# A hybrid layer of Strassen products on one core: a bank of its own for one product, a normalisation on ScalarE, and a sixth slot

## The chip, the core and the metric

The kernel runs on one core of a Trainium2 chip. The metric is the device time of the whole launch in microseconds (us), as the median of several runs; lower is better. A core has five engines with an instruction queue each: TensorE (PE in the rows) multiplies matrices, VectorE (DVE), ScalarE (ACT) and GpSimd (POOL) work elementwise, and SyncE (SP) only issues DMA transfers. Each queue is served in order, so that an instruction that waits holds up all that stand behind it on its engine. TensorE writes its results into eight banks of PSUM, 128 partitions of 512 fp32 each; the others read them there.

## What is computed

One layer over 1024 tokens of 1024 channels, in fp32: a norm, one wide input projection (7680 columns, 512 of them for `v`), three token mixers, three output projections with gates, a last projection, a residual and a norm.

```python
h = _rmsnorm(x, g)                       # 1024 tokens x 1024
parts = h @ w_in                         # u, v, z_A | x_B, B, C, z_B | x_C, z_C | g_A, g_B, g_C
# mixer A: spatial gating in chunks of 128 tokens
u = jax.nn.gelu(u)
v = _layernorm(jax.nn.gelu(v), ln_g, ln_b)
w_m = jnp.where(causal, w_s, 0.0)
sg = jnp.einsum('gts,bnsgc->bntgc', w_m, vc) + b_s.T[:, :, None]
y_A = u * sg                             # then * silu(z_A)
# mixer B: gated convolution over 3 tokens; mixer C: causal pooling over 2, 4, 8, 16 tokens
# each y * silu(z), times its own matrix, times sigmoid(g); the sum times w_out, plus x; last RMSNorm
```

## The kernel before, in words

**Products.** Every fp32 product is three matmuls of a reduced type: each operand is split into a high and a low part (`split_to`: ScalarE casts the high part, VectorE or GpSimd subtracts for the low one), and `mm3` adds high x high, high x low and low x high (lines 90 to 92) in one bank. On top of it stands the Winograd form of Strassen's method: x, transposed, is cut into four blocks A11 to A22 and four combinations S1 to S4, kept split for the whole main loop; the weights of a pair of 128-column blocks are cut likewise, with T1 to T4 worked out on VectorE. A pair then takes seven products instead of eight, listed in `PRODUCTS`, each of 12 matmuls of 512 columns. From pair 2 on (`PLAIN = 2`), the product A12 x B21 of two neighbouring pairs is again done as seven products of half the size, the "j" steps, whose results `p2_q` VectorE puts together (`joint`).

**The main loop** (lines 539 to 623) runs over 28 pairs: ten of gates ("g") and mixer A ("a") in turn, then mixers B and C with the rest of the gates. In rows of an order, `p37` is the bank of the 37th step, `ch43` and `cl43` the split weights of the 43rd, `T1_n5` the first combination of pair 5, and `o0_4`, `o1_4` the two output tiles of pair 4 (128 channels x 1024 tokens). A pair's steps are (A11,B11) into bank `px`, (S1,T1) into `py_`, (S2,T2), (S3,T3), (A22,T4), (S4,B22). `block` adds a bank and another part into half of an output tile and applies the activation. The two places that matter are these:

```python
px = product(("n", 0), more=True)
...
block(o0, lohalf, px, both[p], f0)       # VectorE reads px
...
nc.scalar.copy(out=u2, in_=product(("n", 2), px))   # (S2,T2) is added onto px
```

**Mixer A.** `v` is projected first, and its gelu put to DRAM. In the pair ahead of an "a" pair, `spatial` loads the weights `wsr`, masks them on GpSimd, splits them into `wss` and loads 128 channels of `v` for all tokens as `vr` (eight tiles of 128 x 128); `spatial_norm` subtracts the mean and multiplies by the deviation's inverse `lr` on VectorE (line 467), multiplies and adds the row gain and bias on GpSimd and splits the result into `vh`, `vl`. In the "a" pair, `spatial_mm` multiplies and ScalarE adds the bias into `st`; `gate` transposes `st` on TensorE into the banks `st_0` and `st_1`, multiplies them into `o0` on VectorE and stores it. `gate` is kept as `late` and called near the end of the next pair.

**Order and slots.** A tile scheduler, not the program's text, settles the order on each engine, from the text's order, the slots and a timeline of its own; the order is fixed when the kernel is built. Tiles of one tag share `BUFS[tag]` slots, taken in turn: "q" (512 fp32 a partition) six, "m" (1024 fp32) five. A tile waits until the slot's earlier user is done. The output tiles, `vr`, `vh`, `vl`, `st`, x and, in the last part, the residual rows `res0` to `res7` are all "m".

**The last part** does the output projection for four pairs of 128-token rows, again with seven products; GpSimd adds parts of them into `res` (loaded from x), VectorE adds the last and normalises, and SP stores. The order is `res1`, `res0`, `res3`, `res2`, `res5`, `res4`, `res7`, `res6`; the last one's last quarter is split in two products, `pl0` and `pl1`. Two of the "m" slots hold other tiles then, so three are left for `res`.

## Time and profile before

| | |
|---|---|
| median of 3 runs | 879.81 us (877.88 to 882.89) |
| the profiled execution | 879.07 us; span of its instructions 877.3 us |
| TensorE busy, granted clock | 831.0 us (95% of the span); 0.983 of full on average |
| VectorE busy | 628.5 us (72%) |
| ScalarE busy | 343.4 us (39%) |
| GpSimd busy | 382.0 us (44%) |
| moved by DMA | 99.56 MB, mean 113 GB/s |

Busy shares are averages over stages with different limits. TensorE is the engine to follow here, since it is busy nearly throughout: what counts is where it waits, for whom, and at which clock it works. A granted clock of 1.00 is the full 2.4 GHz, 0.5 would be 1.2 GHz throughout; a value between is a mean over a stretch. An idle time in square brackets is that of the engine just before the instruction, with the one that released it.

### The profile page before, as it was taken

How to read it: one execution, taken by the hardware profiler on the slowest of the kernel's cores; microseconds unless marked ns; L12 is line 12 of the kernel's file. 1: busy time of each engine (PE TensorE's matmuls, PEld its weight loads, DVE VectorE, ACT ScalarE, POOL GpSimd, SP SyncE). 2: the span in 40 equal slices, each digit the busy share in tenths (PEclk: the TensorE clock that was granted, in tenths of full speed). 3: DMA queues.
4: the chain of work that ended last, by engine and by line, in shares of the span. 5: the costliest groups of instructions: out<-in, count | busy, mean ns of one | idle time of the engine just before them, and what ended most of it. 6: DMA issues, size and time to landing. Idle time of an engine off the chain costs nothing.

```text
span 877.3 us, 11162 instructions
## 1 busy us (share of the span) xinstructions
PE 831.0 (95%) x3950; PEld 693.7 (79%) x3950; DVE 628.5 (72%) x1033; ACT 343.4 (39%) x671; POOL 382.0 (44%) x347
## 2 busy tenths in 40 slices
PE   7999989898989999999999999999999999898992
PEld 6787878787878888888888888888878888785882
DVE  6867776777676778769676767777546745797985
ACT  4435434344443424223235444445433301343431
POOL 6743543645555535344452213143000353548874
PEclk9999999999999999999999999999999999999996
DMA  7402332232313122021221313123498553421044
GB/s 288 157 37 72 107 122 96 63 142 61 144 60 145 49 72 96 25 96 49 72 99 49 139 40 140 73 99 121 154 323 294 173 183 113 151 73 48 5 164 143
DMA packets 33879, 99.56 MB, mean 113 GB/s; under 512 B 3488, under 2 KB 9632, under 8 KB 33824
## 3 DMA queue, kind: packets, MB, share of 16 engines
q1 hardware_dynamic: 27920, 83.90, 27.9%
q10 hardware_dynamic: 5904, 14.96, 4.5%
q8 instruction: 31, 0.51, 0.2%
q14 instruction: 24, 0.20, 0.1%
HBM read 73.68 MB, written 25.17 MB: 113 GB/s over the span
## 4 chain that ended last, share of the span: by engine, by line
PE 74%; DVE 11%; DMA 6%; POOL 5%; issue 2%; ACT 2%; POOLq 0%; DVEq 0%; SPq 0%; ACTq 0%
PE p L90 19%; PE p L91 18%; PE p L92 18%; PE py L751 10%; DMA rawo<-in_units_dram 1%; DVE rq L83 1%; DVE vr L467 1%; POOL S_a L83 1%; DMA x<-in_x_dram 1%; POOL res L83 1%; PE pv L92 1%; DVE wss L83 1%; PE pv L90 1%; PE pv L91 1%; PE po L90 1%
## 5 line engine op out<-in xcount | busy, mean ns | idle before, releaser
L83 POOL TENSOR_TENSOR cl<-raw,ch 128x512 fp32r<-128x512 f32 x58 | 82.3, 1421 | 162.5 <-PE p L92 59.2
L83 DVE TENSOR_TENSOR cl<-T_n,ch 128x512 fp32r<-128x512 f32 x112 | 76.2, 682 | 51.4 <-PE p L91 44.9
L86 ACT CAST ch<-T_n 128x512 fp32r<-128x512 f32 x112 | 65.6, 586 | 94.3 <-PE p L91 48.4
L83 DVE TENSOR_TENSOR o<-p,u 128x512 f32<-128x512 f32 x86 | 58.2, 684 | 24.1 <-PE p L92 23.8
L86 ACT CAST ch<-raw 128x512 fp32r<-128x512 f32 x71 | 43.7, 618 | 44.0 <-PE p L91 33.8
L90 PE MATMUL p<-S2h,ch 128*128 128x512 f32 x112 | 46.4, 414 | 12.0 <-DVE o L83 11.6
L83 DVE TENSOR_TENSOR cj<-T_j,cj 128x256 fp32r<-128x256 f32 x52 | 33.3, 642 | 31.9 <-ACT cj L86 31.9
L86 ACT CAST cj<-T_j 128x256 fp32r<-128x256 f32 x52 | 21.1, 406 | 65.5 <-PE p L91 54.6
L91 PE MATMUL p<-S2l,ch 128*128 128x512 f32 x112 | 45.2, 404 | 0.0
L92 PE MATMUL p<-S2h,cl 128*128 128x512 f32 x112 | 45.1, 402 | 0.0
L557 ACT ACTIVATE o<-o 128x512 f32<-128x512 f32 x48 | 30.0, 631 | 37.9 <-DVE o L83 37.7
L90 PE MATMUL p<-A11h,ch 128*128 128x512 f32 x112 | 44.3, 396 | 0.3 <-ACT ch L86 0.3
L92 PE MATMUL p<-A11h,cl 128*128 128x512 f32 x112 | 43.8, 391 | 0.6 <-POOL cl L83 0.6
L90 PE MATMUL p<-A22h,ch 128*128 128x512 f32 x112 | 43.7, 391 | 0.0
L91 PE MATMUL p<-A22l,ch 128*128 128x512 f32 x112 | 43.7, 391 | 0.0
L90 PE MATMUL p<-S3h,ch 128*128 128x512 f32 x112 | 43.7, 391 | 0.0
L90 PE MATMUL p<-S1h,ch 128*128 128x512 f32 x112 | 43.7, 391 | 0.0
L91 PE MATMUL p<-A11l,ch 128*128 128x512 f32 x112 | 43.7, 391 | 0.0
L91 PE MATMUL p<-S1l,ch 128*128 128x512 f32 x112 | 43.7, 391 | 0.0
L91 PE MATMUL p<-S3l,ch 128*128 128x512 f32 x112 | 43.7, 391 | 0.0
L91 PE MATMUL p<-S4l,ch 128*128 128x512 f32 x112 | 43.6, 389 | 0.0
L90 PE MATMUL p<-S4h,ch 128*128 128x512 f32 x112 | 43.6, 389 | 0.0
(474 smaller groups left out, 2543.9 us busy)
## 6 DMA issues: line engine op xcount, KB each, us to landing
raw<-in_units_dram SPq DMA_DIRECT2D x56, 512.0 KB, 3.3
gate<-o ACTq DMA_DIRECT2D x24, 512.0 KB, 2.7
gt<-gate SPq DMA_DIRECT2D x24, 512.0 KB, 4.4
rawp<-in_units_dram SPq DMA_DIRECT2D x12, 512.0 KB, 4.4
yr<-y SPq DMA_DIRECT2D x12, 512.0 KB, 4.5
x<-in_x_dram SPq DMA_DIRECT2D x8, 512.0 KB, 6.7
y<-o SPq DMA_DIRECT2D x8, 512.0 KB, 2.8
rawo<-in_units_dram SPq DMA_DIRECT2D x8, 512.0 KB, 4.0
```

The costliest lines, as they stand in the source:

```text
L83: eng.tensor_tensor(out=o, in0=a, in1=b, op=op)
L86: nc.scalar.copy(out=hi, in_=src)
L90: nc.tensor.matmul(ps, lhsT=wh, rhs=bh, start=first, stop=False, skip_group_check=shared)
L91: nc.tensor.matmul(ps, lhsT=wh, rhs=bl, start=False, stop=False, skip_group_check=shared)
L92: nc.tensor.matmul(ps, lhsT=wl, rhs=bh, start=False, stop=last, skip_group_check=shared)
L467: nc.vector.tensor_scalar(out=vr[:, i, :], in0=vr[:, i, :], scalar1=mv[:, i, 0:1], scalar2=lr[:, i:i + 1], op0=ALU.subtract, op1=ALU.mult)
L557: nc.scalar.activation(out=dst, in_=dst, func=func)
L751: nc.tensor.matmul(py[h], lhsT=w[:, tsl(c)], rhs=yt[b][h][s][:, c, :], start=c == 0 and w is wh and s == 0, stop=c == CT - 1 and w is wl)
```

## The change

1. Product (S2,T2) goes into a bank of its own. ScalarE copies `px` to a new tile `s1`; VectorE adds the bank and `s1` into `u2`.
2. `v` is normalised by ScalarE: eight activations with the scale `lr` and a bias `lb = -mean * lr`, both pointers to a column. `spatial_norm` is called later in the pair's text, after `spatial_mm`.
3. GpSimd's instructions of 1024 columns in this part are cut into two of 512 (`vr`, the product `o0*o1` of mixers A and B, `a`), and so is the split of `vr`. The low part of `wss` moves from VectorE to GpSimd.
4. `gate` and `pool_mm`, where another pair follows and the pair isn't one of the later gates, are called right ahead of product (S2,T2) in the next pair instead of near its end.
5. "m" has six slots; the scratch tile `junk` of the first norm takes one of them for a while.

```diff
@@ -68,7 +68,7 @@
     dram = ctx.enter_context(tc.tile_pool(name="dram", bufs=1, space=bass.MemoryType.DRAM))
     psum = ctx.enter_context(tc.tile_pool(name="psum", bufs=8, space=bass.MemoryType.PSUM))
 
-    BUFS = {"h": 14, "wc": 18, "raw": 4, "T": 3, "q": 6, "m": 5}
+    BUFS = {"h": 14, "wc": 18, "raw": 4, "T": 3, "q": 6, "m": 6}
 
     def slot(tag, name, shape, dtype=F32):
         return big.tile(list(shape), dtype, name=name, tag=tag, bufs=BUFS[tag])
@@ -174,7 +174,7 @@
         hb[name] = tuple(slot("h", f"{name}{c}", (P, KH, HALF), F32R) for c in "hl")
     v_dram = dram.tile([P, NT, CW], F32, name="v_dram")
     parts = {}
-    junk = const.tile([P, D], mybir.dt.bfloat16, name="junk")
+    junk = slot("m", "junk", (P, D), mybir.dt.bfloat16)
 
     def norm(n):
         i = TOKENS[n]
@@ -441,6 +441,8 @@
     ahead(-1)
     lr = const.tile([P, NT], F32, name="lr")
     rsqrt(mv[:, :, 1], 1.0, LN_EPS, (2, slice(0, NT)), lr)
+    lb = const.tile([P, NT], F32, name="lb")
+    nc.vector.scalar_tensor_tensor(out=lb, in0=mv[:, :, 0], scalar=-1.0, in1=lr, op0=ALU.mult, op1=ALU.mult)
 
     gates = [dram.tile([P, S], F32, name=f"gate{n}") for n in range(24)]
     ys = [[dram.tile([P, S], F32, name=f"y{b}_{j}") for j in range(CT)] for b in range(3)]
@@ -454,7 +456,7 @@
                                 base=0, channel_multiplier=-1)
         wss = slot("q", f"wss{j}", (P, 2, 2 * P), F32R)
         src = wsr.rearrange("p g t -> p (g t)")
-        split_to(wss[:, 0, :], wss[:, 1, :], src)
+        split_to(wss[:, 0, :], wss[:, 1, :], src, nc.gpsimd)
         for r in range(2):
             lo = r * CW + j * P
             nc.scalar.dma_start(out=lnr[:, r, :], in_=rows[0:1, lo:lo + P].broadcast_to([P, P]))
@@ -464,13 +466,15 @@
 
     def spatial_norm(j, wss, lnr, vr):
         for i in range(NT):
-            nc.vector.tensor_scalar(out=vr[:, i, :], in0=vr[:, i, :], scalar1=mv[:, i, 0:1], scalar2=lr[:, i:i + 1],
-                                    op0=ALU.subtract, op1=ALU.mult)
-        tt(nc.gpsimd, vr, vr, lnr[:, 0:1, :].to_broadcast([P, NT, P]), ALU.mult)
-        tt(nc.gpsimd, vr, vr, lnr[:, 1:2, :].to_broadcast([P, NT, P]), ALU.add)
+            nc.scalar.activation(out=vr[:, i, :], in_=vr[:, i, :], func=AF.Identity, bias=lb[:, i:i + 1],
+                                 scale=lr[:, i:i + 1])
         vh = slot("m", f"vh{j}", (P, NT, P), F32R)
         vl = slot("m", f"vl{j}", (P, NT, P), F32R)
-        split_to(vh, vl, vr)
+        for half in range(2):
+            c = tsl(half, KH)
+            tt(nc.gpsimd, vr[:, c], vr[:, c], lnr[:, 0:1, :].to_broadcast([P, KH, P]), ALU.mult)
+            tt(nc.gpsimd, vr[:, c], vr[:, c], lnr[:, 1:2, :].to_broadcast([P, KH, P]), ALU.add)
+            split_to(vh[:, c], vl[:, c], vr[:, c])
         return wss, vh, vl
 
     def spatial_mm(j, wss, vh, vl):
@@ -562,36 +566,40 @@
 
         u2 = slot("q", f"u2_{p}", (P, HALF))
         u3 = slot("q", f"u3_{p}", (P, HALF))
-        px = product(("n", 0), more=True)
+        s1 = slot("q", f"s1_{p}", (P, HALF))
+        px = product(("n", 0))
+        nc.scalar.copy(out=s1, in_=px)
         if nxt[0] == "a":
             sp_next = spatial(nxt[1])
         then(0)
         if p < PLAIN:
-            nc.scalar.copy(out=u2, in_=px)
-            block(o0, lohalf, product(("n", 1)), u2, f0)
+            block(o0, lohalf, product(("n", 1)), s1, f0)
             if p == PLAIN - 1:
                 cut_again(False)
         else:
             block(o0, lohalf, px, both[p], f0)
         py_ = product(("n", 4), more=True)
         then(4)
-        nc.scalar.copy(out=u2, in_=product(("n", 2), px))
+        if late is not None and nxt[0] is not None and not (kind == "g" and j >= 6):
+            late()
+            late = None
+        tt(nc.vector, u2, product(("n", 2)), s1, ALU.add)
         then(2)
         tt(nc.vector, u3, product(("n", 3)), u2, ALU.add)
         block(o1, hihalf, py_, u3, f1)
         then(3)
         if p == 0:
             cut_again(True)
-        if nxt[0] == "a":
-            sp_next = spatial_norm(nxt[1], *sp_next)
         block(o0, hihalf, product(("n", 5)), u3, f0)
         if kind == "g":
             nc.scalar.dma_start(out=gates[2 * j], in_=o0)
         then(5)
         if kind == "a":
             st = spatial_mm(j, *sp)
+        if nxt[0] == "a":
+            sp_next = spatial_norm(nxt[1], *sp_next)
         sp = sp_next
-        if late is not None:
+        if late is not None and kind == "g" and j >= 6:
             late()
             late = None
         block(o1, lohalf, product(("n", 6), py_), u2, f1)
@@ -600,10 +608,12 @@
         if kind == "g":
             nc.scalar.dma_start(out=gates[2 * j + 1], in_=o1)
         elif kind == "a":
-            tt(nc.gpsimd, o0, o0, o1, ALU.mult)
+            for hs in (lohalf, hihalf):
+                tt(nc.gpsimd, o0[:, hs], o0[:, hs], o1[:, hs], ALU.mult)
             late = lambda j=j, st=st, o0=o0: gate(j, st, o0)
         elif kind == "b":
-            tt(nc.gpsimd, o1, o0, o1, ALU.mult)
+            for hs in (lohalf, hihalf):
+                tt(nc.gpsimd, o1[:, hs], o0[:, hs], o1[:, hs], ALU.mult)
             a = slot("m", f"a{j}", (P, S))
             nc.vector.tensor_scalar(out=a, in0=o1, scalar1=cw[:, 3 * j + 2:3 * j + 3], scalar2=cb[:, j:j + 1],
                                     op0=ALU.mult, op1=ALU.add)
@@ -614,8 +624,9 @@
             conv[j] = a
         elif kind == "bz":
             a = conv[j]
-            tt(nc.gpsimd, a, a, o0, ALU.mult)
-            tt(nc.gpsimd, a, a, o1, ALU.mult)
+            for o in (o0, o1):
+                for hs in (lohalf, hihalf):
+                    tt(nc.gpsimd, a[:, hs], a[:, hs], o[:, hs], ALU.mult)
             nc.sync.dma_start(out=ys[1][j], in_=a)
         elif kind == "c":
             pool_weights(j)
```

What this does to the order of instructions, at three places. The first is pair 4 on TensorE, where (S2,T2) begins; before, it followed the half-size product with S1:

```order
L91 MATMUL p40_1668<-S1l_again_959,cj40_1536 128x256
L92 MATMUL p40_1668<-S1h_again_958,cj40_1536 128x256
L90 MATMUL p37_1604<-S2h_141,ch41_1562 128x512
L91 MATMUL p37_1604<-S2l_142,ch41_1562 128x512
L92 MATMUL p37_1604<-S2h_141,cl41_1563 128x512
```

and after the change:

```order
L91 MATMUL p40_1687<-S1l_again_963,cj40_1552 128x256
L92 MATMUL p40_1687<-S1h_again_962,cj40_1552 128x256
L493 MATMUL st0_0_1695<-ident_80,st0_1565 128x128 x4
L493 MATMUL st0_1_1701<-ident_80,st0_1565 128x128 x4
L90 MATMUL p41_1714<-S2h_141,ch41_1578 128x512
L91 MATMUL p41_1714<-S2l_142,ch41_1578 128x512
L92 MATMUL p41_1714<-S2h_141,cl41_1579 128x512
```

The transposes of pair 3's gate now stand ahead of (S2,T2), which writes `p41` instead of adding onto `p37`.

The same stretch on VectorE before: `vr1` is the tile of `v` for the next pair, `o0_4<-p37` the read of `px`:

```order
L467 TENSOR_SCALAR vr1_1625<-vr1_1625,mv_131,lr_804 128x128 x4
L83 TENSOR_TENSOR o1_3_1402<-p28_1431,u2_3_1403 128x512
L467 TENSOR_SCALAR vr1_1625<-vr1_1625,mv_131,lr_804 128x128 x4
L83 TENSOR_TENSOR cl43_1601<-T3_n4_1598,ch43_1600 128x512
L83 TENSOR_TENSOR p2_5_1485<-p36_1585,p2_5_1485 128x256
L83 TENSOR_TENSOR cl44_1630<-T4_n4_1627,ch44_1629 128x512
L83 TENSOR_TENSOR T1_n5_1676<-raw7_1539,raw6_1249 128x512
L83 TENSOR_TENSOR p2_4_1484<-p38_1637,p2_5_1485 128x256
L83 TENSOR_TENSOR wss1_1620<-wsr1_1617,wss1_1620 128x256
L83 TENSOR_TENSOR o0_4_1594<-p37_1604,p2_4_1484 128x512
L83 TENSOR_TENSOR p2_5_1485<-p40_1668,p2_5_1485 128x256
L83 TENSOR_TENSOR cl47_1679<-T1_n5_1676,ch47_1678 128x512
```

and after:

```order
L83 TENSOR_TENSOR cl44_1649<-T4_n4_1646,ch44_1648 128x512
L83 TENSOR_TENSOR T1_n5_1708<-raw7_1555,raw6_1257 128x512
L83 TENSOR_TENSOR o0_4_1611<-p37_1622,p2_4_1500 128x512
L83 TENSOR_TENSOR p2_5_1501<-p40_1687,p2_5_1501 128x256
L83 TENSOR_TENSOR o0_3_1414<-st0_1_1701,o0_3_1414 128x512
L83 TENSOR_TENSOR cl47_1711<-T1_n5_1708,ch47_1710 128x512
L83 TENSOR_TENSOR T2_n5_1728<-raw7_1555,T1_n5_1708 128x512
L83 TENSOR_TENSOR T3_n5_1741<-raw7_1555 128x512
L83 TENSOR_TENSOR u2_4_1613<-p41_1714,s1_4_1615 128x512
L83 TENSOR_TENSOR p2_5_1501<-p40_1687,p2_5_1501 128x256
L83 TENSOR_TENSOR cl48_1731<-T2_n5_1728,ch48_1730 128x512
L83 TENSOR_TENSOR o0_3_1414<-st0_0_1695,o0_3_1414 128x512
```

The tiles of `vr1` and the split of `wss1` are gone from VectorE, the addition `u2_4` is new, and the gate's two products from `st0_1` and `st0_0` stand between the splits and combinations of the next weights.

The second place is SP's queue at the end, before:

```order
L783 DMA res3_7024<-in_x_dram 128x1024
L843 DMA out_dram<-res1_7022 128x1024
L843 DMA out_dram<-res0_7020 128x1024
L783 DMA res2_7188<-in_x_dram 128x1024
L783 DMA res5_7222<-in_x_dram 128x1024
L843 DMA out_dram<-res3_7024 128x1024
L783 DMA res4_7360<-in_x_dram 128x1024
L843 DMA out_dram<-res2_7188 128x1024
L783 DMA res7_7420<-in_x_dram 128x1024
L843 DMA out_dram<-res5_7222 128x1024
L843 DMA out_dram<-res4_7360 128x1024
L783 DMA res6_7558<-in_x_dram 128x1024
```

and after:

```order
L794 DMA res3_7140<-in_x_dram 128x1024
L794 DMA res2_7304<-in_x_dram 128x1024
L854 DMA out_dram<-res1_7138 128x1024
L794 DMA res5_7338<-in_x_dram 128x1024
L854 DMA out_dram<-res0_7136 128x1024
L794 DMA res4_7476<-in_x_dram 128x1024
L854 DMA out_dram<-res3_7140 128x1024
L794 DMA res7_7536<-in_x_dram 128x1024
L854 DMA out_dram<-res2_7304 128x1024
L794 DMA res6_7674<-in_x_dram 128x1024
L854 DMA out_dram<-res5_7338 128x1024
L854 DMA out_dram<-res4_7476 128x1024
```

`res2` now follows `res3` with no store between, and each later load moves ahead of one or two stores.

The third is the start on VectorE, where x0 and x4 (the first rows of the two halves) are normalised, before:

```order
L112 TENSOR_SCALAR norms_130<-tmp_66 128x1
L188 SCALAR_TENSOR_TENSOR x0_69<-x0_69,norms_130,ng0_72 128x512
L188 SCALAR_TENSOR_TENSOR x0_69<-x0_69,norms_130,ng1_73 128x512
L102 TENSOR_SCALAR tmp_66<-norms_130 128x1
L83 TENSOR_TENSOR A11l_134<-pt_0_0_165,A11h_133 128x4x128
L105 TENSOR_SCALAR tmp_66<-tmp_66 128x1
L109 TENSOR_SCALAR tmp_66<-tmp_66 128x1
L112 TENSOR_SCALAR norms_130<-tmp_66 128x1
L253 CAST wvh4_204<-rawv2_103 128x512
```

and after:

```order
L112 TENSOR_SCALAR norms_130<-tmp_66 128x1
L102 TENSOR_SCALAR tmp_66<-norms_130 128x1
L188 SCALAR_TENSOR_TENSOR x0_69<-x0_69,norms_130,ng0_72 128x512
L188 SCALAR_TENSOR_TENSOR x0_69<-x0_69,norms_130,ng1_73 128x512
L105 TENSOR_SCALAR tmp_66<-tmp_66 128x1
L109 TENSOR_SCALAR tmp_66<-tmp_66 128x1
L253 CAST wvh4_204<-rawv2_103 128x512
L112 TENSOR_SCALAR norms_130<-tmp_66 128x1
L253 CAST wvh5_208<-rawv2_103 128x512
L188 SCALAR_TENSOR_TENSOR x4_99<-x4_99,norms_130,ng0_72 128x512
L188 SCALAR_TENSOR_TENSOR x4_99<-x4_99,norms_130,ng1_73 128x512
L83 TENSOR_TENSOR A11l_134<-pt_0_0_165,A11h_133 128x4x128
```

The first step of the second norm (line 102) now stands ahead of the scaling of `x0_69` (line 188), and the split `A11l` of its transposes behind that of `x4_99`.

## Rows read from the trace of the kernel before

**Rows 1.** the waits of TensorE: engine, result, line, releaser: us in total, times, longest.

```profile
PE p L90 <- DVE o L83: 11.8, 5, 3.5
...
PE pv L92 <- DVE A21l L83: 1.8, 1, 1.8
PE po L90 <- ACT ah L86: 1.6, 1, 1.6
```

**Rows 2.** the page, part 5: busy us, mean ns, then idle us before, and releaser.

```profile
L90 PE MATMUL p<-S2h,ch 128*128 128x512 f32 x112 | 46.4, 414 | 12.0 <-DVE o L83 11.6
```

**Rows 3.** busy time by stretches: stretch, length, engines, then TensorE's granted clock, DMA share, GB/s.

```profile
130.00:160.00 30.00, 30.00 (x145) 25.28 (x144) 19.61 (x33) 14.13 (x26) 10.80 (x10) 1.00 0.24 84
160.00:175.00 15.00, 11.46 (x53) 9.54 (x52) 10.16 (x17) 4.87 (x9) 10.60 (x8) 0.89 0.23 68
...
205.00:217.00 12.00, 9.30 (x48) 7.84 (x47) 9.68 (x18) 4.35 (x9) 7.69 (x5) 0.94 0.31 94
217.00:250.00 33.00, 33.00 (x159) 27.76 (x158) 22.25 (x35) 15.05 (x30) 16.49 (x14) 0.97 0.30 109
250.00:262.00 12.00, 9.21 (x47) 7.73 (x46) 9.38 (x17) 4.25 (x8) 8.06 (x6) 0.91 0.24 75
...
832.00:877.00 45.00, 29.60 (x142) 24.80 (x141) 32.30 (x78) 12.20 (x36) 24.95 (x27) 0.86 0.43 152
```

**Rows 4.** timeline of VectorE and TensorE in pair 4: start, us, engine, line [idle before].

```profile
161.56 1.90 DVE L467 TENSOR_SCALAR vr<-vr,mv,lr 128x128 f32<-128x128 f32 x4 [1.59 <-DMA vr<-v_dram]
...
168.24 0.41 DVE L83 TENSOR_TENSOR p<-p,p 128x256 f32<-128x256 f32 x1
168.57 2.22 DVE L83 TENSOR_TENSOR wss<-wsr,wss 128x256 fp32r<-128x256 f32 x1
...
170.72 0.68 DVE L83 TENSOR_TENSOR o<-p,p 128x512 f32<-128x512 f32 x1
...
171.45 0.80 PE L90 MATMUL p<-S2h,ch 128*128 128x512 f32 x1 [3.54 <-DVE o L83]
```

**Rows 5.** timeline of SP, ScalarE and GpSimd in pair 4.

```profile
157.36 0.52 SPq L462 DMA_DIRECT2D vr<-v_dram  x1
...
164.10 0.63 ACT L552 ACTIVATE sg<-o 128x512 f32<-128x512 f32 x1 [2.38 <-DVE o L83]
...
167.57 2.94 POOL L83 TENSOR_TENSOR vr<-vr,wsr 128x1024 f32<-128x1024 f32 x1 [0.77 <-DVE p L83]
...
170.47 2.55 POOL L83 TENSOR_TENSOR o<-o,o 128x1024 f32<-128x1024 f32 x1
```

**Rows 6.** the chain that ended last, 854 to 877: start, us, what.

```profile
855.75 4.54 DMA out_dram<-res
...
860.30 3.31 DMA res<-in_x_dram
```

**Rows 7.** timeline of SP, TensorE and VectorE from 852 to 870.

```profile
852.31 0.34 SPq L843 DMA_DIRECT2D out_dram<-res  x1
...
861.32 0.28 PE L92 MATMUL pl<-r,al 128*128 128x256 f32 x1
...
868.67 0.75 DVE L83 TENSOR_TENSOR res<-pl,res 128x256 f32<-128x256 f32 x2
```

**Rows 8.** groups of instructions by line: busy us, mean ns, idle before.

```profile
L467 DVE TENSOR_SCALAR vr<-vr,mv,lr 128x128 f32<-128x128 f32 x32 | 13.1, 471 | 4.7 <-DMA vr<-v_dram 4.7
...
L86 ACT CAST ah<-mg 128x128 fp32r<-128x128 f32 x48 | 11.4, 294 | 15.8 <-DVE mg L83 15.8
...
L482 ACT ACTIVATE st<-sg,sm 128x512 f32<-128x512 f32 x8 | 5.5, 694 | 0.0
```

**Rows 9.** timeline of VectorE, ScalarE and TensorE from 8 to 30.

```profile
8.93 3.43 DVE L188 SCALAR_TENSOR_TENSOR x<-x,norms,ng 128x512 f32<-128x512 f32 x2
9.82 1.06 ACT L184 ACTIVATE junk<-x 128x1024 bf16<-128x1024 f32 x1 [0.50 <-DMA x<-in_x_dram]
...
29.47 0.48 PE L90 MATMUL pv<-wvh,A11h 128*128 128x512 f32 x1
```

## The prediction

> **What bounds the kernel now.** I read the table of busy shares first. TensorE is busy 831.0 of 877.3 us, so any gain must come from its 46 idle us or from stretches in which it runs at a lower clock; VectorE (628.5) and GpSimd (382.0) matter only where TensorE waits for them. The list of TensorE's waits says where that is: one entry, a matmul of line 90 behind VectorE's `o`, holds 11.8 us in five waits [rows 1]. The table of instruction groups puts 11.6 of them on one product, (S2,T2) [rows 2]. In TensorE's timeline these are four waits of 2.6 to 3.5 us, at 128, 171, 216 and 260 us; the one at 171.45 is shown [rows 4]. They lie in pairs 2, 4, 6 and 8, the pairs just ahead of an "a" pair, in which `spatial_norm` runs.
>
> The idle time isn't all. The table by stretches shows the granted clock at 0.89, 0.94, 0.97 and 0.91 in the stretches that hold or follow the last three of those waits, and 1.00 just before them [rows 3]; width times missing clock is 15 x 0.11 = 1.65, 12 x 0.06 = 0.72, 33 x 0.03 = 0.99 and 12 x 0.09 = 1.08 us, together 4.4. So the four stalls cost about 16.0 us.
>
> Why there: VectorE's timeline at pair 4 [rows 4]. It waits 1.59 us for the load of `vr1`, normalises its eight tiles in two runs of four (the first takes 1.90 us), and then spends 2.22 us on the split `wss`, an instruction that on a tile of the same size takes 0.41 us beside it. Only then comes `o<-p,p` at 170.72, the read of px; TensorE starts (S2,T2) 0.73 us later, at 171.45. The wait exists because (S2,T2) accumulates onto the bank that `o<-p,p` reads. The `wss` split ends at 170.79, with the end of GpSimd's 2.94 us multiplication of `vr` (167.57 to 170.51) [rows 5].
>
> The end of the span is the second place. TensorE's last matmul starts at 861.32 and lasts 0.28 us [rows 7], yet the span goes on to 877.3. The chain that ended last shows why: the store of `res4` and `res5`, issued 855.75, must land before `res6` may be loaded into a slot (issue 860.30, landing 863.6), and two additions by GpSimd follow [rows 6]; VectorE adds the two last quarter products only at 868.67 and, 0.34 later, at 869.01 [rows 7].
>
> **The change, part by part.** *S2 in a bank of its own.* The wait on `o<-p,p` is removed; nothing that TensorE now needs comes behind `vr` and `wss` in the same way. ScalarE copies px to `s1` instead of the sum to `u2`, the same 28 copies, and VectorE gets 28 additions of 128x512 from a bank, 0.68 us each by `o<-p,p` [rows 4]: +19.0 us of VectorE. Against it go 32 x 471 ns = 15.1 (busy 13.1, since they overlap) for `vr` [rows 8] and four `wss` of 2.2, 8.9. VectorE's total changes by about -3 us in 628, so it doesn't become the bound. If the wait goes, the clock loss that followed it goes too, as I read it, because pairs without such a gap show 1.00. Term: **-16.0**. Bounds: -11.6 if the clock still falls for other reasons, and 0 if the waits come back in another form (rival C).
>
> *The normalisation on ScalarE.* `vr` is issued at 157.36 and lands at 161.5 as before [rows 5]; now ScalarE stands behind it, with the cast `ch43` behind eight activations. No row shows a 128x128 activation with two pointer operands. From below: a cast of that size, 294 ns; from above: an activation four times as wide with one pointer, 694 ns [rows 8]. Eight of them are 2.4 to 5.6 us; I take the lower part, 0.3 to 0.45 us each, since the price of 294 is for the same size, and hence an end at about 164 to 165. TensorE without its stall reaches (S2,T2) at 171.45 - 3.54 = 167.9, spends 12 x 0.227 = 2.7 on it plus 0.9 for the transposes that now stand before it and 0.7 for the half-size product, and wants `ch43` at about 172.2: 7 us of cover. The other thing behind it on ScalarE, the sigmoid of `o1` (now at 164.10 [rows 5]), moves by 1 to 2 us. Term: 0.
>
> The Trainium skill, page "ScalarE: Activation LUTs", section "Rules for kernel authors", advises VectorE and not ScalarE for additions and multiplications, VectorE being up to about three times as fast (it says so of bf16). That speaks against this edit. By the row the term is 0; by that rule, with the factor taken over to fp32 here, it would be the 18.8 us of rival D.
>
> *GpSimd's halves and the early gate.* The order shows what VectorE meets: `o0_3<-st0_1` and `o0_3<-st0_0` now stand ahead of `cl47` and `T4_n5`, and (S3,T3) takes over a bank from the first. The gate's product `o0*o1` must be done by then. It ended at 170.47 + 2.55 = 173.0 [rows 5]. Worked out for pair 4: sigmoid ending about 165.5, `o1*sg` 1.3, first half 1.3 (168.1), the mask 0.4, two halves of `vr` at half of the 2.55 of such an instruction of full width (171.0), one `cl` 1.3, second half 1.3: about 174. TensorE needs what stands behind the second half at the start of (S1,T1), 172.2 + 2 x 2.7 = 177.6. Cover: 3.6 us. The moved `wss` stands behind these on GpSimd and is wanted a pair later. The gate's store and its DMA wait on SP leave earlier, not later. Term: 0.
>
> *Slots: m from 5 to 6.* SP's order of the tail shows that `res2` now loads at once and that `res6` comes right behind the store of `res2`, where it came behind those of `res5` and `res4`: its slot is `res2`'s instead. The store of `res2` is issued at 852.31 now [rows 7], late because `res2` itself was loaded late. Were it no earlier, `res6` would be issued at 852.31 + 4.54 = 856.9 and land at 860.2 instead of 863.6, a gain of 3.4; loaded at once it leaves several us earlier, and the last addition can follow the last matmul's end, 861.6, instead of standing at 869.01, a gain of 7.4. The 8.3 us from there to the end (877.3 - 869.01) stay. What limits it next is VectorE: from 832 to the end it is busy 32.3 us [rows 3], some 3.5 of them behind the last addition, so that without any wait it would get there at 832 + 28.8 = 860.8, only 0.8 us ahead of TensorE. I take **-6.5**; bounds -3.4 and -8.5 (the norms' additions at the end run beside GpSimd's products now, and may not then).
>
> *Smaller ones.* The wait of 1.6 us for `ah` in the tail [rows 1] goes, for the most part, because GpSimd's parts of `S_a` come in another order: **-1.2** (0 to -1.7). The start gets worse. VectorE's norm of `x0` starts at 8.93 now; in the new order it stands behind the first step of `x4`'s norm, and `x4`'s sum of squares runs on ScalarE from 9.82 to 10.98 [rows 9]: +2.2 us, and the split of x0's first transposes stands behind `x4`'s norm as well. I expect the second v product, at 29.47 now [rows 9], about 3.5 us later. Part comes back: the wait of 1.8 us on `A21l` [rows 1], at 40.9, is for work that a later TensorE finds done. Net **+1.5** (-0.5 to +4).
>
> **Sum.** The profiled execution took 879.07 us, 1.8 more than its span and 0.7 less than the median of the three runs, 879.81. 879.07 - 16.0 - 6.5 - 1.2 + 1.5 = **856.9 us**. Other waits in the main loop I leave as they are.
>
> **Rivals.** *A, the forecast*: chance 0.55, 852 to 862 (the start's range and the tail's).
> *B, the tail isn't shorter*: another load or GpSimd's queue sets the last addition, at the old distance. For it: GpSimd is busy 25 of the last 45 us [rows 3]; against it: `res6` is loaded at least 3.4 us earlier. 856.9 + 6.5 = 863.4; chance 0.13.
> *C, the waits return as others*: (S2,T2) needs a bank that someone must have emptied, and (S3,T3) one that the early gate empties; px's old bank frees no earlier. If half of the 16 us returns at the same four pairs, 864.9; with the start at its worst 867.4. Against it: the cover of 3.6 to 7 us above. Chance 0.20.
> *D, no gain that can be measured*: ScalarE is much slower at this than VectorE. If an activation of 128x128 takes 1.41 us, twice the 694 ns of the one four times as wide, eight end at 161.5 + 11.3 = 172.8. Then cast, sigmoid and GpSimd's five pieces put the second half of `o0*o1` at about 182.3, 4.7 us behind 177.6, at each of four pairs: 18.8 us. 856.9 + 18.8 = 875.7, at the edge of no change. The 294 ns speak against it. Chance 0.06. (1.41 is also three times VectorE's 471 ns, which is what the rule of the Trainium skill's page "ScalarE: Activation LUTs", section "Rules for kernel authors", would give as an estimate.)
> *E, slower than before*: the same place, VectorE's queue held by `o0_3<-st0_0` with the `cl` and `T` of the next products behind it, decides only if the second half of `o0*o1` ends later than about 177.6 + 7 = 184.6 at all four pairs: 4 x 7 = 28 us turn 856.9 into 884.9, and a clock that falls behind such gaps, as it did behind shorter ones [rows 3], adds the same 4 us again: 889. Nothing in the rows asks so much. Chance 0.04.
> That the tail stays and the waits half return together has the remaining 0.02 (871.4).
>
> A measurement of this kernel tells a change from none at about 0.5%, 4.4 us: 875.4 and 884.2 are the bounds. Faster: A, B, C and the last, 0.90; same: D, 0.06; slower: E, 0.04. The range reaches from the forecast with the best tail and start and other small waits gone too, 849, to C with the worst start and a little beyond, 868.
>
> **What would show it.** Right: the entry "p L90 <- DVE o" nearly gone from the waits; clock 1.00 from 160 to 335; eight activations of `vr` in 2.4 to 3.6 us a pair; `res6` landing ahead of the last matmul; 8 to 9 us from that to the end. Wrong: a new wait of 1 us or more at (S3,T3) or (S1,T1) of pairs 4, 6, 8, with VectorE's `o<-st` as releaser; a second v product later than 33.5 with the wait at 40.9 still there; a tail of 12 us or more.

## The result, and the profile after

The changed kernel takes 856.88 us (median of 4 runs, 856.46 to 857.04), against 880.52 us for four runs of the one before: ratio 0.9732, 95% interval 0.9702 to 0.9761. Forecast were 856.9 us. The total came out to the microsecond; three of its four terms did not, since the main loop gave more than was worked out and the end less.

The profiled execution took 857.04 us, its span 855.2. TensorE's timeline can be cut at three marks: the first matmul of the main loop, the first of the merge (`py`), and the last one of all. The main loop is what lies between the first two, the last part what lies between the next two, the tail what follows the last matmul's start. "Busy in it" is TensorE's busy time in the stretch to its left, and the rest of that stretch is its idle time. The medians were taken on four occasions (changed; the r_ kernels; x_bank, v_junkwc, n5 and n6; x_norm, y_raw6 and z_raw6), and each ratio goes by runs of the kernel before on the same occasion. The other columns are those of one profiled execution each. This table carries most of what follows:

| kernel | median us | main loop starts | main loop | busy in it | last part | busy in it | tail | span |
|---|---|---|---|---|---|---|---|---|
| before | 880.52 | 76.03 | 567.85 | 552.07 | 217.44 | 210.60 | 15.95 | 877.27 |
| changed | 856.88 | 77.36 | 546.33 | 545.23 | 219.71 | 213.50 | 11.76 | 855.16 |
| r_bank | 864.11 | 77.25 | 551.78 | 548.02 | 221.31 | 212.71 | 11.74 | 862.08 |
| r_norm | 856.71 | 77.21 | 546.28 | 545.19 | 219.71 | 211.05 | 11.92 | 855.12 |
| r_m6 | 854.78 | 75.71 | 546.29 | 545.18 | 215.43 | 209.89 | 15.75 | 853.18 |
| r_late | 857.35 | 77.19 | 546.05 | 545.05 | 221.61 | 212.45 | 10.49 | 855.34 |
| x_bank | 854.66 | 75.96 | 545.85 | 545.04 | 214.90 | 209.75 | 16.41 | 853.12 |
| x_norm | 860.59 | 75.72 | 550.48 | 546.83 | 217.35 | 209.29 | 15.52 | 859.07 |
| v_junkwc | 855.32 | 78.21 | 546.28 | 545.16 | 219.49 | 210.88 | 11.92 | 855.90 |
| n5 | 854.20 | 75.70 | 546.32 | 545.17 | 214.95 | 208.59 | 15.42 | 852.39 |
| n6 | 849.15 | 73.64 | 546.32 | 545.21 | 219.32 | 210.87 | 7.94 | 847.22 |
| y_raw6 | 852.98 | 75.92 | 545.63 | 545.01 | 215.07 | 208.59 | 14.41 | 851.03 |
| z_raw6 | 854.57 | 78.88 | 545.64 | 545.01 | 215.10 | 208.53 | 14.36 | 853.98 |

Changed against before: start +1.33, main loop -21.52, last part +2.27, tail -4.19, together -22.1 us, the difference of the spans. In the main loop TensorE's idle time fell from 15.8 to 1.1 us and its busy time by 6.8 us.

TensorE's waits in the changed kernel (in total, times, longest), the answer to [rows 1]:

```profile
PE pt L194 <- DVE x L188: 7.0, 2, 6.0
PE po L92 <- DVE tmp L109: 2.2, 1, 2.2
PE py L762 <- ACT ph__6747 L86: 1.8, 1, 1.8
...
PE po L90 <- ACT ah L86: 1.2, 1, 1.2
...
PE p L92 <- POOL cl L83: 0.6, 1, 0.6
```

The entry "p L90 <- DVE o" is gone. The main loop keeps one wait of 0.6 us, in its first pair, and one of 0.3 us; the other waits lie at the start and in the last part. The group of (S2,T2) from the page, the answer to [rows 2], has lost its 11.6 us:

```profile
L90 PE MATMUL p<-S2h,ch 128*128 128x512 f32 x112 | 44.1, 393 | 0.0
```

In the table by stretches, over the same time as [rows 3] (columns as there), TensorE is busy throughout and its granted clock never leaves 1.00:

```profile
110.00:130.00 20.00, 20.00 (x109) 17.33 (x108) 11.89 (x23) 11.67 (x25) 4.62 (x6) 1.00 0.44 143
130.00:175.00 45.00, 45.00 (x223) 38.16 (x222) 33.56 (x53) 23.65 (x47) 31.03 (x26) 1.00 0.28 89
175.00:217.00 42.00, 42.00 (x210) 35.65 (x210) 30.82 (x50) 22.92 (x46) 27.86 (x26) 1.00 0.36 123
217.00:262.00 45.00, 45.00 (x224) 38.16 (x223) 33.15 (x53) 24.77 (x50) 27.19 (x24) 1.00 0.37 120
262.00:335.00 73.00, 72.88 (x365) 61.84 (x364) 54.20 (x85) 27.17 (x51) 37.72 (x31) 1.00 0.24 80
```

Three groups that the change makes, from the table by line: the new additions, the activations and the moved split.

```profile
L83 DVE TENSOR_TENSOR u<-p,s 128x512 f32<-128x512 f32 x28 | 19.0, 679 | 1.7 <-PE p L92 1.7
...
L469 ACT ACTIVATE vr<-vr,lb,lr 128x128 f32<-128x128 f32 x32 | 12.7, 484 | 0.0
...
L83 POOL TENSOR_TENSOR wss<-wsr,wss 128x256 fp32r<-128x256 f32 x4 | 4.8, 1193 | 0.0
```

The activation with two pointer operands took 484 ns (mean of 32), inside the bounds of 294 and 694 ns [rows 8], a little over the 0.3 to 0.45 us that I took. The Trainium skill, page "ScalarE: Activation LUTs", section "What ACT_TABLE_LOAD costs", gives 186 ns plus 0.833 ns a column plus about 93 ns for each pointer operand, an estimate of 479 ns at 128 columns; the trace agrees. The same split `wss` that took 2.2 us on VectorE beside a GpSimd instruction took 1.2 us on GpSimd.

### The profile page after: what moved, and what is told of

The parts are those of the page before. It is cut to its first block, busy times and chain, and to the rows that moved or that the text cites. A ratio compares the mean times of both kernels' runs of the same rounds, so it can differ in the third digit from the quotient of the medians.

```text
span 855.2 us, 11281 instructions
## 1 busy us (share of the span) xinstructions
PE 826.8 (97%) x3950; PEld 693.6 (81%) x3950; DVE 632.8 (74%) x1030; ACT 354.3 (41%) x705; POOL 391.9 (46%) x375
## 5 line engine op out<-in xcount | busy, mean ns | idle before, releaser
L83 DVE TENSOR_TENSOR p<-p,p 128x256 f32<-128x256 f32 x78 | 32.4, 416 | 19.6 <-PE p L92 19.4
L90 PE MATMUL p<-S4h,ch 128*128 128x512 f32 x112 | 43.9, 392 | 0.5
L90 PE MATMUL p<-A11h,ch 128*128 128x512 f32 x112 | 43.9, 392 | 0.3 <-ACT ch L86 0.3
L90 PE MATMUL p<-S2h,ch 128*128 128x512 f32 x112 | 44.1, 393 | 0.0
L90 PE MATMUL p<-S1h,ch 128*128 128x512 f32 x112 | 43.7, 391 | 0.0
L90 PE MATMUL p<-A22h,ch 128*128 128x512 f32 x112 | 43.7, 391 | 0.0
L90 PE MATMUL p<-S3h,ch 128*128 128x512 f32 x112 | 43.7, 390 | 0.0
L92 PE MATMUL p<-S4h,cl 128*128 128x512 f32 x112 | 43.6, 389 | 0.0
```

The source lines that it names most:

```text
L83: eng.tensor_tensor(out=o, in0=a, in1=b, op=op)
L90: nc.tensor.matmul(ps, lhsT=wh, rhs=bh, start=first, stop=False, skip_group_check=shared)
L92: nc.tensor.matmul(ps, lhsT=wl, rhs=bh, start=False, stop=last, skip_group_check=shared)
```

## The experiments

First one part at a time was taken out of the changed kernel (r_), then one part at a time was put alone into the kernel before (x_), and then the end was taken apart.

**r_bank**: without the bank for (S2,T2).

```diff
-        s1 = slot("q", f"s1_{p}", (P, HALF))
-        px = product(("n", 0))
-        nc.scalar.copy(out=s1, in_=px)
+        px = product(("n", 0), more=True)
...
-        tt(nc.vector, u2, product(("n", 2)), s1, ALU.add)
+        nc.scalar.copy(out=u2, in_=product(("n", 2), px))
```

> The changed kernel (856.9) with only the bank undone: (S2,T2) is again added onto px's bank, ScalarE copies the sum, VectorE's 28 additions u2 go. The start and the slots stay as in the changed kernel. Theory K (the shared bank is the cause of the four waits): they come back wholly or for the most part, +8 to +16 us, 865 to 873, with 'p L90 <- DVE o' at 6 us or more. Theory N (VectorE's hold behind vr and wss was the cause, and px is read in time once these are gone): the four waits stay under 0.5 us each, 856 to 859. Between them: the waits of 0.5 to 0.6 us ahead of S3's half-size product, which the changed kernel lost, come back, +1.5 to +4.5.

Measured: 864.11 us (ratio to before 0.9824, interval 0.9803 to 0.9846), 7.2 more than the changed kernel. The four waits did not come back: no "p L90 <- DVE o" is among its waits. The main loop is 5.5 us longer: TensorE idles 2.7 us more in it and is busy 2.8 us more. The two rows show the largest of the small waits (in total, times, longest). A wait costs more than its idle time here: in steady work the next matmul starts 0.227 us after the last, which still takes 0.39, so by estimate some 0.16 us of overlap is lost at each; this explains a part of the busy time, and the rest isn't resolved.

```profile
PE p L90 <- ACT ch L86: 1.8, 5, 0.4
...
PE pp L90 <- ACT u L585: 1.1, 2, 0.7
```

The last part is 1.6 us longer too, which makes up the rest. So theory N holds for the four waits, but the time is far from N's 856 to 859, and just below K's 865 to 873. The case between them said 1.5 to 4.5 us, by waits ahead of S3's half-size product; these aren't in the list, others are. The bank is worth 5.5 us of main loop even where VectorE isn't held.

**r_norm**: without the moved normalisation and `wss`.

```diff
-            nc.scalar.activation(out=vr[:, i, :], in_=vr[:, i, :], func=AF.Identity, bias=lb[:, i:i + 1],
-                                 scale=lr[:, i:i + 1])
+            nc.vector.tensor_scalar(out=vr[:, i, :], in0=vr[:, i, :], scalar1=mv[:, i, 0:1], scalar2=lr[:, i:i + 1],
+                                    op0=ALU.subtract, op1=ALU.mult)
...
-        split_to(wss[:, 0, :], wss[:, 1, :], src, nc.gpsimd)
+        split_to(wss[:, 0, :], wss[:, 1, :], src)
```

> The changed kernel with the normalisation of v and the low part of wss back on VectorE, all else as changed. Theory K (a bank of its own suffices): TensorE doesn't wait at (S2,T2) any more, 856 to 859. Theory N (VectorE's hold is what costs): the hold of about 4 us for vr and 2 us for wss stays, and what is late next is the read of px as a bank for a later product or the split cl43 and the gate's multiplications ahead of (S3,T3): waits of 1 to 3 us in pairs 2, 4, 6, 8 and 861 to 869.

Measured: 856.71 us, main loop 546.28 against 546.33. Theory K. With a bank of its own for (S2,T2), VectorE may work on `vr` and `wss` as before; nothing else is late in the main loop.

**r_m6**: five "m" slots, `junk` in its own place.

```diff
-    BUFS = {"h": 14, "wc": 18, "raw": 4, "T": 3, "q": 6, "m": 6}
+    BUFS = {"h": 14, "wc": 18, "raw": 4, "T": 3, "q": 6, "m": 5}
...
-    junk = slot("m", "junk", (P, D), mybir.dt.bfloat16)
+    junk = const.tile([P, D], mybir.dt.bfloat16, name="junk")
```

> The changed kernel with five m slots and junk in its own place again. The order at the start is then the old one, and the loads of res at the end too. My terms: the start comes back by 1.3 us (the main loop began 1.33 us later in the changed kernel), the tail behind the last matmul gets 4.2 us longer (15.95 against 11.76), the output projection's new wait of 2.2 us on VectorE perhaps goes, so 857.0 - 1.3 + 4.2 - 2 to 0 = 857.9 to 859.9. Rival: the slots are worth nothing on the whole, since what they save behind the last matmul is lost ahead of it: 854 to 857. Second rival: the sixth slot also carried the main loop (vr, vh, st and the output tiles are m tiles), and without it waits come back there: over 862.

Measured: 854.78 us (854.25 to 855.20), 2.1 us faster than the changed kernel; the rival held. The table says how: the sixth slot takes 4.0 us off the tail, and adds 4.3 to the last part and 1.6 to the start.

**r_late**: gate and pooling products late again.

```diff
-        if late is not None and nxt[0] is not None and not (kind == "g" and j >= 6):
-            late()
-            late = None
...
-        if late is not None and kind == "g" and j >= 6:
+        if late is not None:
```

> The changed kernel with the gate's transposes and the pooling's products again near the end of the next pair. My reading: the early call hides nothing that was on the path in mixer A's pairs, but the two waits ahead of the pooling's products (0.56 and 0.84 us in the kernel before) were lost with it, so +0 to +2 us, 857 to 859. Rival: the early multiplications hold VectorE for GpSimd's product and cost something, so that the late call is faster, 854 to 856. Second rival: without the early gate the output tiles hold m slots longer and loads come late, over 861.

Measured: 857.35 us (857.06 to 857.46), 0.5 more than the changed kernel. The main loop is the same to 0.3 us, so the two waits ahead of the pooling's products had not been lost through the early call, as I had read it (x_bank, which has no early call, lacks them too); the last part is 1.9 us longer and the tail 1.3 shorter.

**x_bank**: the kernel before, with the bank alone (the diff of r_bank read the other way).

> The kernel before with one part alone: (S2,T2) in a bank of its own, s1 copied by ScalarE, u2 added by VectorE. Since the changed kernel without the moved normalisation keeps its whole gain (856.7) and the main loop is 546.1 us long in it, theory K (the bank alone suffices) has the main loop at 546 to 547.5 us here too, 20 us shorter, and the time at 880.2 - 20 = 859 to 861, with start and end as before. Theory N2 (the bank suffices only where the gate's early call and GpSimd's halves keep the next waits away): VectorE's hold of 6 us turns up as waits ahead of (S3,T3), 862 to 868.

Measured: 854.66 us (854.03 to 856.15; ratio to before 0.9712, interval 0.9698 to 0.9727). This one part gives the whole gain of the change and, by medians of two occasions, 2 us more; both theories had it slower. The main loop is 22.0 us shorter, 2 more than expected, and the last part 2.5 us shorter, which nothing had forecast. TensorE has only these two waits left over 0.2 us in the main loop:

```profile
PE p L92 <- POOL cl L83: 0.6, 1, 0.6
PE p L90 <- ACT ch L86: 0.3, 1, 0.3
```

VectorE still normalises `vr` and splits `wss` in this kernel, GpSimd's instructions are whole, and the gate is called late, so theory N2 is out.

**x_norm**: the kernel before, with the normalisation on ScalarE and `wss` on GpSimd alone (the diff of r_norm the other way, with `lb`).

> The kernel before with the normalisation of v on ScalarE and the low part of wss on GpSimd, and nothing else: (S2,T2) still adds onto px's bank. Theory N (VectorE's hold of 4 us for vr and 2 us for wss is what made px late): the four waits of 2.6 to 3.5 us go, the main loop is 550 to 552 us long as in the changed kernel without the bank (551.56), and the time is 880.3 - 15 to -16 = 864 to 866. Theory K only (the bank is needed): 872 or more.

Measured: 860.59 us (ratio 0.9781, interval 0.9737 to 0.9824), 3 to 5 below the expected. Main loop 550.48: 17.4 us shorter. The four waits are gone as theory N says; what remains against the bank's 545.85 are the small waits that the kernel before had as well:

```profile
PE p L90 <- ACT p L429: 1.3, 3, 0.4
...
PE pp L90 <- ACT u L580: 1.1, 2, 0.7
```

So either part removes the four waits, and only the bank removes these. TensorE idles 2.8 us more than in x_bank and is busy 1.8 us more. Whether the normalisation or `wss` held the read of `px` wasn't tried apart.

**v_junkwc**: six slots, with `junk` elsewhere.

```diff
-    junk = slot("m", "junk", (P, D), mybir.dt.bfloat16)
+    junk = slot("wc", "junk", (P, D), mybir.dt.bfloat16)
```

> The changed kernel with six m slots, but the scratch tile junk among the split weights' slots (tag wc) instead of an m slot. The order at the start is the old one then. Theory J (junk in an m slot delays the start, the sixth slot as such is worth about 4 us at the end and costs as much ahead of it): main loop begins at 75.7 and the time is 856.9 - 1.6 = 855.3, give or take 0.7. Theory M (junk's place is harmless, the sixth slot itself costs the start): main loop begins at 77.4 and 856.9.

Measured: 855.32 us as a median, but of two kinds: 853.2, 853.3, 857.4 and 858.0. The profiled execution is the slowest of these, with the main loop starting at 78.21; n6, whose order at the start is the same, starts it at 73.64. Its median is theory J's, but no execution was near it. The two first norms run in the old order again, so `junk` did move them; the order isn't the old one throughout, though: SP issues four loads of x in a row from 6.66 on, where the kernel before issues three, and the same holds for n6. Last part and tail are those of the changed kernel, so they go with the sixth slot, not with `junk`.

**n5, n6**: five and six slots (r_m6 and v_junkwc), with less work for VectorE. For six of the eight row tiles the multiplication by the final gain is left out.

```diff
-                    nc.vector.scalar_tensor_tensor(out=o[:, hs], in0=o[:, hs], scalar=rs, in1=fg[:, hs],
-                                                   op0=ALU.mult, op1=ALU.mult)
+                    nc.scalar.mul(out=o[:, hs], in_=o[:, hs], mul=rs)
```

> The changed kernel with five m slots (854.8), and six of the eight row tiles are scaled by ScalarE alone, without the final norm's gain (left out for these rows): 12 instructions of some 0.75 to 1.2 us leave VectorE in the output projection. Theory V (VectorE's work sets the end of the last part, whatever slots there are): 3 to 8 us shorter, 847 to 852, by fewer waits of TensorE there and a shorter way behind its last matmul. Theory L (the loads of the residual tiles set the end with five slots: each waits for a store that waits for the tile before): the tail behind the last matmul stays at 14 us or more and the time falls by under 2.5 us, 852.3 to 855.

> The same work left out (final gain of six row tiles), with six m slots and junk among the split weights. Theory V: VectorE was the limit, so it gains as much as or more than the five-slot kernel does from the same step: 846 to 851, tail behind the last matmul about 8.5 to 9.5 us. Theory L: with six slots no load is late, so the step gains at most the 1 to 2 us by which VectorE was behind at the end: 853 to 855.

Measured: n5 854.20 us, 0.6 less than r_m6, tail 15.42 against 15.75. n6 849.15 us; by stages, which leave its earlier start aside, it differs from v_junkwc by the tail alone, 7.94 against 11.92. With five slots the loads set the end (theory L), with six it is VectorE (theory V). The chain of n5 (start, us, what) shows the store, the load that waits for it, and GpSimd's additions behind the load, just as in [rows 6]:

```profile
830.35 5.00 DMA out_dram<-res
...
835.37 3.37 DMA res<-in_x_dram
...
838.89 2.48 POOL res L83 x2
```

and the timeline of n6 shows the addition of the last quarter product 0.3 us behind the last matmul's start, with VectorE idle ahead of it:

```profile
839.28 0.28 PE L92 MATMUL pl<-r,al 128*128 128x256 f32 x1
...
839.60 0.42 DVE L83 TENSOR_TENSOR res<-pl,res 128x256 f32<-128x256 f32 x1 [0.72 <-PE pl L92]
```

But the last part stayed at 219.3 us in n6. Its timeline shows why: the scaling, now ScalarE's (line 851), stands ahead of the cast `ah` that TensorE waits for.

```profile
799.58 1.33 ACT L851 ACTIVATE res<-res,norms 128x512 f32<-128x512 f32 x2 [0.41 <-DVE tmp L102]
...
801.43 1.12 ACT L86 CAST ah<-S_a 128x512 fp32r<-128x512 f32 x2
...
802.08 0.50 PE L90 MATMUL po<-rq,ah 128*128 128x512 f32 x1 [2.76 <-ACT ah L86]
```

**y_raw6**: x_bank, with `res6` alone in a slot of another tag; five "m" slots.

```diff
-            res[i] = slot("m", f"res{i}", (P, D))
+            res[i] = slot("raw" if i == NT - 2 else "m", f"res{i}", (P, D))
```

> The kernel before with the bank for (S2,T2) alone (854.7), and the last residual tile res6 in a slot of the tag raw, which the output projection's weights have left by then; five m slots as before. Theory O (the sixth m slot cost time because residual work of early rows came ahead of the splits that the next products wait for, not because res6 came early): no wait is added ahead of the last matmul, 620 to 837 as in that kernel, and the tail falls from 16.4 us to about 12, the 11.8 of the changed kernel: 850 to 851.5. Theory P (an early res6 itself brings that work forward): TensorE's last matmul comes 2 to 4 us later and the time stays at 853 to 856.

Measured: 852.98 us (852.69 to 854.00), 1.7 us below x_bank (854.03 to 856.15, timed on another occasion), but above theory O's 850 to 851.5. The last part is that of x_bank to 0.2 us, so theory O holds there: an earlier `res6` as such costs TensorE nothing. But the last two loads of residual rows start only 2 and 5 us earlier than in x_bank, and the tail fell by 2.0 us only, to 14.41. Its timeline (start, us, engine) has the next things in line:

```profile
827.85 2.82 SPq L784 DMA_DIRECT2D res<-in_x_dram  x2
...
831.52 2.45 DVE L841 SCALAR_TENSOR_TENSOR res<-res,norms,fg 128x512 f32<-128x512 f32 x2
...
831.82 1.60 POOL L83 TENSOR_TENSOR res<-res,os 128x512 f32<-128x512 f32 x1 [1.90 <-DMA res<-in_x_dram]
...
842.43 0.75 DVE L83 TENSOR_TENSOR res<-pl,res 128x256 f32<-128x256 f32 x2
```

`res7`, still an "m" tile, and `res6` are loaded one behind the other from 827.85 on, and GpSimd waits for the first to land, until 831.8; VectorE is scaling earlier tiles until 834.0. The quarter products are added at 842.43, 5.8 us behind the start of the last matmul (836.62).

**z_raw6**: y_raw6, with part of the scaling moved to ScalarE and GpSimd.

```diff
+                elif h and i >= 2:
+                    nc.scalar.mul(out=o[:, hs], in_=o[:, hs], mul=rs)
+                    tt(nc.gpsimd, o[:, hs], o[:, hs], fg[:, hs], ALU.mult)
```

> The same, and from row tile 2 on the second half of each of the middle row tiles is scaled by ScalarE and multiplied by the gain on GpSimd instead of both on VectorE: four instructions of 0.75 to 1.2 us leave VectorE, four of 0.7 us go to ScalarE and four of 1.3 to GpSimd. With six slots and 12 such instructions gone the tail fell by 4.0 us, to 7.9; a third of that is 1.3 us. Theory V: 849 to 850.5, tail 10.5 to 11. Rival: GpSimd's 5 us come ahead of its splits S_a, and TensorE waits for these: 851 to 854.

Measured: 854.57 us (853.32 to 855.69), far from theory V's 849 to 850.5 and just above the rival's 851 to 854. Last part 215.10 and tail 14.36 are the same as in y_raw6; the profiled execution started its main loop 3 us later. By stages neither theory V's gain nor the rival's wait is there, which fits an end that the late load of `res7` sets, not VectorE's work ahead of it; that wasn't tried alone.

## Why the total was right, point by point

**The bank: -16.0 forecast.** The four waits and the clock went, as said. x_norm, which removes them and leaves the other small waits, makes the main loop 17.4 us shorter: 12.1 of idle and 5.2 of busy time. So the sum over waits and missing clock was 1.4 short; half of that is the stretch behind the last wait, which I had left out (73 x 0.01 = 0.7):

```profile
262.00:335.00 73.00, 73.00 (x362) 61.80 (x361) 52.50 (x75) 28.08 (x53) 36.05 (x27) 0.99 0.22 80
```

The failed step is the sentence "Other waits in the main loop I leave as they are": they went too, 4 to 5 us of them (545.85 to 546.33 against 550.48), and only with the bank. A likely account, not shown, is that px's bank was held from its product to ScalarE's copy of the sum behind (S2,T2), so that later products and the pooling's got their banks late; the runs show only that these waits come and go with the bank. The main loop's real term was -21.5. The bank also shortens the last part, by 2.5 us (x_bank against before) or 1.6 (changed against r_bank); I had no term for that, and why it does so is open.

I had put the whole cause on the shared bank, and the runs bear that out more strongly than the argument did: with it, the other edits to the main loop are worth nothing measurable (r_norm, r_late, and x_bank, which has none of them). But VectorE's hold was a cause as well: without it the shared bank is read in time. The two stand in a row, and to remove either is enough. VectorE's total went up by 4.3 us, to 632.8, where I had -3; the main loop's share fell by 1.0, the last part's rose by 5.2.

**The normalisation: 0 forecast, 0 measured.** ScalarE's timeline in pair 4 and what waits behind it:

```profile
147.82 0.53 SPq L464 DMA_DIRECT2D vr<-v_dram  x1
...
156.26 3.19 ACT L469 ACTIVATE vr<-vr,lb,lr 128x128 f32<-128x128 f32 x8
...
160.35 0.62 ACT L556 ACTIVATE sg<-o 128x512 f32<-128x512 f32 x1
...
163.05 1.29 POOL L83 TENSOR_TENSOR o<-o,o 128x512 f32<-128x512 f32 x1
...
166.27 0.48 PE L90 MATMUL p<-S2h,ch 128*128 128x512 f32 x1
...
168.87 1.29 POOL L83 TENSOR_TENSOR o<-o,o 128x512 f32<-128x512 f32 x1
...
173.41 0.67 DVE L83 TENSOR_TENSOR o<-st,o 128x512 f32<-128x512 f32 x1
```

The eight activations take 3.19 us, as priced, from 156.26 on. But the working had `vr` issued at 157.36 "as before" [rows 5], and that was wrong: with six slots it is issued at 147.82, so ScalarE never waits for it. The 0 doesn't hang on that: in r_m6, with five slots, ScalarE waits 8.5 us for `vr` in all, the activations of this pair end at 161.66, and the main loop is as long (546.29). The sigmoid of `o1` starts at 160.35, the second half of `o0*o1` ends at 170.16 and VectorE reads it at 173.41. (S1,T1) starts at 178.01, three products behind (S3,T3) at 169.82 and not two as in my sum, so the cover is 7.8 us where I worked out 3.6. Rivals D and E had this product end at 182.3 us and later. Twice the 694 ns of D is 1.39 us, and not 1.41, which changes nothing. By the rows the price is nearly the same on both engines: 484 ns on ScalarE, 471 ns on VectorE [rows 8]. The rule of the Trainium skill's page "ScalarE: Activation LUTs", section "Rules for kernel authors", prefers VectorE for additions and multiplications by a factor that it states for bf16; carried over to fp32, as in D, the factor isn't borne out here.

**The slots: -6.5 forecast, -4.2 measured** in the tail, inside the bounds of -3.4 and -8.5, with VectorE as the next limit, as said (n6). The tail was to be 8 to 9 us long and is 11.8, since the last addition doesn't follow the last matmul's end. `res6` is issued at 829.16, 14 us ahead of the last matmul, and the quarter products are added 3.2 us behind it (846.56 and 846.90 against 843.40):

```profile
829.16 0.33 SPq L794 DMA_DIRECT2D res<-in_x_dram  x1
...
843.40 0.28 PE L92 MATMUL pl<-r,al 128*128 128x256 f32 x1
...
846.56 0.75 DVE L83 TENSOR_TENSOR res<-pl,res 128x256 f32<-128x256 f32 x2
```

The step that failed stands in the next term: **-1.2 forecast for the wait on `ah`, +2.3 measured** for the last part. The wait on `ah` went from 1.6 to 1.2 us only, and the term had nothing else in it. By r_m6, which has all but the slots, the last part is 2.0 us shorter than before; the sixth slot adds 4.3. With an early `res2` the finished row tiles came earlier in VectorE's queue too, and one of them, scaled at 803.33, stands ahead of the split `al` that TensorE waits for:

```profile
803.33 2.40 DVE L851 SCALAR_TENSOR_TENSOR res<-res,norms,fg 128x512 f32<-128x512 f32 x2
...
806.43 0.68 DVE L83 TENSOR_TENSOR al<-S_a,ah 128x512 fp32r<-128x512 f32 x1
...
807.16 0.50 PE L92 MATMUL po<-rq,al 128*128 128x512 f32 x1 [2.21 <-DVE tmp L109]
```

In r_m6 the order is the other way round; its split `al` runs at 797.43, ahead of the first scalings at 807.30:

```profile
797.43 1.34 DVE L83 TENSOR_TENSOR al<-S_a,ah 128x512 fp32r<-128x512 f32 x1
...
807.30 2.94 DVE L851 SCALAR_TENSOR_TENSOR res<-res,norms,fg 128x512 f32<-128x512 f32 x4
```

The wait of 2.2 us isn't the whole of the 4.3. Against r_m6 TensorE idles only 0.7 us more in this execution and is busy 3.6 us more, because its granted clock fell to the lower level three times in the last part, each time behind 1.6 to 2.2 us of waits, and in r_m6 once, behind 1.8. By the granted clock each fall costs 5 x 0.34 = 1.7 us, so the two more cost 3.4. In the table by stretches (columns as in [rows 3]) the changed kernel has

```profile
729.00:734.00 5.00, 4.95 (x15) 3.91 (x16) 3.95 (x8) 1.12 (x3) 1.05 (x1) 0.66 0.44 130
784.00:789.00 5.00, 5.00 (x17) 3.95 (x16) 3.35 (x5) 4.57 (x15) 5.00 (x6) 0.66 0.00 0
808.00:813.00 5.00, 5.00 (x17) 3.94 (x16) 5.00 (x12) 3.77 (x15) 5.00 (x9) 0.66 0.36 116
```

and r_m6

```profile
772.00:777.00 5.00, 5.00 (x16) 3.99 (x15) 1.37 (x3) 1.87 (x5) 3.54 (x4) 0.66 0.30 105
```

r_norm and v_junkwc, with six slots too, have one such fall each, at their wait of 2.4 us on the split, and idle 8.6 to 8.7 us instead of 6.2; their last parts are as long to 0.2 us. So the length goes with the slots, and only its division into waits and lower clock changes. r_m6 and v_junkwc show that it belongs to the sixth slot (215.43 against 219.71 and 219.49), and y_raw6 speaks against the earlier load of `res6` as such. That it is the scaling, and not another piece of early residual work, is read from these rows and from n6, where the wait moved with the scaling to ScalarE; it wasn't tried alone. So the slots and what hangs on them, start included, cost 2 us, where my terms made -6.2 of them (-6.5 - 1.2 + 1.5).

**The start: +1.5 forecast, +1.33 measured**, by the mechanism given:

```profile
10.35 1.05 ACT L184 ACTIVATE junk<-x 128x1024 bf16<-128x1024 f32 x1
...
11.64 1.56 DVE L188 SCALAR_TENSOR_TENSOR x<-x,norms,ng 128x512 f32<-128x512 f32 x2
...
12.59 1.12 PE L194 MATMUL pt<-ident,x 128*128 128x128 f32 x4 [6.05 <-DVE x L188]
...
32.35 0.41 PE L90 MATMUL pv<-wvh,A11h 128*128 128x512 f32 x1
```

The norm of `x0` runs behind the sum of squares of `x4` (10.35 on ScalarE) at 11.64 instead of 8.93, and the second v product starts at 32.35, 2.9 us later instead of 3.5; the wait on `A21l` is gone. I had not said why the order changed: it is `junk` in an "m" slot, since r_m6 and v_junkwc have the norms in the old order.

So the errors were -5.5 in the main loop against +2.3 and +3.5 at the end. That they cancel to 0.3 us is chance; the range, made for errors of this size, is what the forecast was worth.

## What to carry to other kernels

When a product accumulates onto a bank that another engine still has to read, a delay of that reader becomes a wait of TensorE; a bank of its own and one more addition on an engine with slack took 22 us off the main loop here by itself. Price the waits that you don't mean to touch as well, if they hang on the same resource. One more slot isn't free where a scheduler orders the queues: what comes earlier may stand ahead of what is needed first, so try it apart from the rest; giving the one late tile a slot that had become free elsewhere kept TensorE's pace, took 2 us off the tail and made the fastest complete kernel here, 853.0 us.

## What I had not expected of the hardware

Kernels with one and the same order of instructions at the start begin their main loop at times 3 to 5 us apart: 73.64 (n6) and 78.21 (v_junkwc), or 75.92 (y_raw6) and 78.88 (z_raw6), which have the order of the kernel before. The four times of v_junkwc fall into two pairs 4 us apart. In both late cases TensorE waited for VectorE's `A21l`, 2.5 us at 41.5 in v_junkwc and 3.0 us at 42.2 in z_raw6, where n6 doesn't wait and y_raw6 waits 1.3 us; why it was late is open.

The times of the four kernels with the new order at the start (changed, r_bank, r_norm, r_late) spread over 0.4 to 0.6 us, those of the others over 0.8 (n5) to 6.7 (the kernel before, on one occasion). So the order that costs 1.3 to 1.6 us in most executions may also steady the start. That isn't shown, since only one execution of each kernel has a profile.
